# Masks of a stick-breaking attention on TensorE, its steps reordered, and later loads of spilled blocks, in a kernel for one hybrid decoder layer

## The chip, the cores and the metric

One core of one Trainium2 chip runs the whole layer as one program. The metric is the device time of one execution in microseconds (us). The engines are named as in the profile: PE (TensorE, products), PEld (its weight loads), DVE (VectorE), ACT (ScalarE), POOL (GpSimd) and SP (SyncE, which here only issues transfers).

## The reference

The layer works on 512 tokens of 2048 features in float32:

```
h    = RMSNorm(x);  u, v_sgu, q, k, v, g_a, g_b = split(h @ W_in)
y_a  = gelu(u) * (tril(W_s) @ RMSNorm(gelu(v_sgu)) + b)       # chunks of 128 tokens, 8 groups
z    = q k^T * scale                                          # 8 heads of 128, q and k normalised
log_1m = where(strict, log_sigmoid(-z), 0)                    # strict: key before query
tail = reverse cumsum over keys of log_1m, less log_1m itself
w    = where(strict, exp(log_sigmoid(z) + tail), 0);  y_b = w @ v
x   += (sigmoid(g_a) * (y_a @ W_up_a) + sigmoid(g_b) * (y_b @ W_up_b)) @ W_o
x   += (silu(gate) * up) @ W_ffn_out,  gate, up = split(RMSNorm(x) @ W_ffn_in)   # 5632 hidden
x   += sigmoid(RMSNorm(x) @ W_gate) * (p @ W_ple)
```

The mask `strict` acts twice: on log_1m before the cumulative sum, and on w after the exponential.

## The kernel before

Features lie on the 128 partitions and tokens on the free axis, so a *block* is 256 features by 512 tokens, stored as 128 x 1024. A large product reads *units* of 256 input features. Each float32 operand is split into a high part (ACT copies it, rounded, to the type fp32r) and a low part (DVE subtracts the high part), and a product is three products hi x hi, hi x lo, lo x hi in PSUM. Weights: `whi` (ACT, L336) and `wlo` (DVE, L333). Inputs: `parts` (ACT L262, DVE L263). A unit of kind P is plain: twelve PE products of 128 x 512. A unit of kind S uses a Strassen-like scheme with seven small products in place of eight, and wants sums of quarter blocks first (DVE L501; ACT L488 multiplies by the norm's gain). The prepared form of a unit is a *form*.

The stages, in order of time: the form of x and the first q, k and v blocks; the other w_in pairs in four rounds (q, k, v and some gate blocks each), then SGU blocks; the up products and W_o; FFN-in with 44 hidden pairs; FFN-out in three passes over the hidden units (`PASSES`), each of 8 output blocks; the gate stage, with the per-layer embedding. Between stages, blocks are spilled to DRAM: y, gates, x1 (after W_o), hid (hidden units), sum (running FFN-out sums), x2 (after the FFN). The first pair of a stage is done *plain*, unit by unit, while the forms of its inputs are still being made.

All engines' orders are written out by a planner in the kernel. Its clock counts *ticks*, one after each unit of a pair: 8 in a pair of W_in. `after(n, f)` runs f n ticks later; `beside(steps, first)` starts a chain of steps, and each `yield n` in it puts the next step n ticks on. Attention is such a chain, so its instructions stand between the large products. `builds` is the list of forms to be made, whose loads and splits are handed out by the ticks. SBUF for blocks is an arena (`wholes`, float32) with `take` and `give`; `parts` is another arena. A block that is reused is only free for writing when what reads it, a store too, has ended.

Attention for one round has two heads. For each of four query/key chunks j, `stage_a` computes z (L1028), log-sigmoids from Abs, Exp and Ln, and zeroes the masked part of log_1m with a POOL affine_select (L1041). `stage_b` splits it (ACT L262, DVE L263, tile `sp`), multiplies both parts by a triangle of ones `tri` on PE (L1056, L1057: the cumulative sum), takes Exp, and zeroes w with a second select (L1063). `finish` multiplies w by v (L1072). Before it, q_prep, k_prep, v_prep and, for SGU, sgu_v normalise blocks: `times` (L987) scales a transposed block, and a transpose (L965) or a product (L1126) reads it. A pair's output block is put together by ACT and DVE, L691 and L694 (in PSUM's place), in a *home* block; the home of a q block also receives y, which is stored from there.

## Time and profile before

| what | value |
|---|---|
| median of 3 timed runs | 2743.61 us (2743.32 to 2745.96) |
| profiled execution | 2738.06 us, span 2736.3 us |
| PE busy | 2680.7 us (98%), granted clock 0.992 |
| DVE busy | 2168.8 us (79%) |
| ACT busy | 1362.4 us (50%) |
| POOL busy | 443.4 us (16%) |
| moved by DMA | 527.82 MB, mean 193 GB/s |

Stage borders on the profile's clock, to find a window: first products until about 87 us, W_in with attention and SGU to 855, up products and W_o to 1195, FFN-in to 2050, FFN-out passes from about 2050, 2245 and 2395, gate stage from 2550. A row of the windows view gives a stretch's length, then each engine's busy time with its count of instructions in brackets, then the granted clock of PE, the share of busy DMA engines and GB/s. A row of the waits view reads "engine tile line <- engine tile line": the second ended the idle time of the first, with the total, the number of times and the longest.

### The profile page before, as it was taken

The numbers are of one execution on the slowest core, as the hardware profiler recorded it, in microseconds if no ns is written. First come the engines' busy times: TensorE is split into PE (matmuls) and PEld (weight loads), VectorE is DVE, ScalarE is ACT, GpSimd is POOL, SyncE is SP. The second block draws the span as 40 slices with busy tenths as digits, with TensorE's granted clock in tenths as the row PEclk, the third lists the DMA queues.
The fourth block names the chain that finished last, engine by engine and source line by source line (L and its number), as shares of the span: only waits on it lengthen the run. The fifth ranks groups of instructions, "written<-read, shape, count | busy, mean of one in ns | idle before, by whom it ended". The sixth has DMA issues, their size and how long they took to land.

```text
span 2736.3 us, 43138 instructions
## 1 busy us (share of the span) xinstructions
PE 2680.7 (98%) x15875; PEld 2360.9 (86%) x15875; DVE 2168.8 (79%) x3713; ACT 1362.4 (50%) x2142; POOL 443.4 (16%) x503
## 2 busy tenths in 40 slices
PE   8999999999999999999999999999999999999899
PEld 6889888888988889988888888888888989988798
DVE  7687878788887667679898989898988577778676
ACT  7756556565544334365444444444445344444443
POOL 0222222222210000001111111111111111010110
PEclk9999999999999999999999999999999999999999
DMA  6677676767776457668888888888887668777784
GB/s 217 160 187 173 170 178 168 176 163 190 172 178 210 137 156 218 176 197 210 220 214 205 203 203 201 203 202 203 202 202 211 172 186 226 199 238 217 212 235 124
DMA packets 302547, 527.82 MB, mean 193 GB/s; under 512 B 25600, under 2 KB 162816, under 8 KB 302336
## 3 DMA queue, kind: packets, MB, share of 16 engines
q1 hardware_dynamic: 241584, 424.65, 49.6%
q0 software_dynamic: 60752, 100.43, 23.2%
q8 instruction: 124, 2.03, 0.3%
q14 instruction: 87, 0.71, 0.1%
HBM read 477.79 MB, written 47.19 MB: 192 GB/s over the span
## 4 chain that ended last, share of the span: by engine, by line
PE 85%; DVE 5%; DMA 4%; ACT 2%; issue 2%; POOL 1%; ACTq 0%; DVEq 0%; SPq 0%; POOLq 0%
PE ps L648 38%; PE ps L268 13%; PE ps L267 13%; PE ps L269 13%; PE small L648 4%; DVE wlo L333 2%; ACT whi L336 1%; DMA wholes<-w_in 1%; DVE out L694 1%; DVE parts L263 1%; PE small L1072 1%; PE small L965 1%; DMA wholes<-x 1%; DVE wholes L501 1%; DMA wholes<-y 0%
## 5 line engine op out<-in xcount | busy, mean ns | idle before, releaser
L336 ACT ACTIVATE whi<-wholes 128x512 fp32r<-128x512 f32 (+4 forms) x950 | 846.5, 916 | 836.0 <-PE ps L268 317.2
L648 PE MATMUL ps<-parts,whi 128*128 128x512 f32 x3384 | 1132.3, 400 | 5.8 <-DVE wholes L694 4.4
L333 DVE TENSOR_TENSOR wlo<-wholes,whi 128x512 fp32r<-128x512 f32 (+4 forms) x950 | 961.0, 1045 | 97.9 <-ACT whi L336 97.2
L267 PE MATMUL ps<-parts,whi 128*128 128x256 f32 (+1 forms) x2675 | 857.1, 323 | 28.0 <-ACT parts L262 13.9
L268 PE MATMUL ps<-parts,whi 128*128 128x256 f32 (+1 forms) x2640 | 858.1, 325 | 3.1 <-DVE parts L263 3.0
L269 PE MATMUL ps<-parts,wlo 128*128 128x256 f32 (+1 forms) x2640 | 854.4, 324 | 0.9 <-DVE wlo L333 0.9
L648 PEld LDWEIGHTS ps<-parts,wlo 128*128 128x128 f32 x3384 | 637.2, 189 | 145.1 <-DVE wlo L333 1.4
L648 PE MATMUL ps<-parts,wlo 128*128 128x256 f32 x3384 | 673.1, 280 | 0.5 <-DVE wlo L333 0.5
L267 PEld LDWEIGHTS ps<-parts,whi 128*128 128x128 f32 x2675 | 510.0, 191 | 73.6 <-ACT parts L262 17.7
L648 PEld LDWEIGHTS ps<-parts,whi 128*128 128x128 f32 x3384 | 544.1, 190 | 11.0 <-DVE wholes L694 4.8
L268 PEld LDWEIGHTS ps<-parts,whi 128*128 128x128 f32 x2640 | 503.5, 191 | 49.7 <-DVE parts L263 5.7
L269 PEld LDWEIGHTS ps<-parts,wlo 128*128 128x128 f32 x2640 | 503.0, 191 | 39.4 <-DVE wlo L333 1.3
L352 DVE TENSOR_TENSOR wholes<-wholes 128x256 f32<-128x256 f32 (+1 forms) x794 | 328.0, 413 | 22.9 <-issue 3.0
L340 POOL DMA_DIRECT2D wholes<-w_ffn_in x172 | 150.1, 872 | 745.5 <-DMA wholes<-w_ffn_in 183.0
L694 DVE TENSOR_TENSOR out<-out,ps 128x256 f32<-128x256 f32 x373 | 152.8, 420 | 116.4 <-ACT out L691 106.3
L340 POOL DMA_DIRECT2D wholes<-w_in x132 | 117.7, 892 | 541.2 <-DMA wholes<-w_in 226.2
L263 DVE TENSOR_TENSOR parts<-wholes,parts 128x1024 fp32r<-128x1024 f32 (+3 forms) x129 | 122.6, 964 | 28.4 <-ACT parts L262 28.0
L648 PE MATMUL small<-parts,whi 128*128 128x512 f32 x344 | 136.0, 395 | 0.0
L262 ACT ACTIVATE parts<-wholes 128x1024 fp32r<-128x1024 f32 (+3 forms) x129 | 105.6, 845 | 53.1 <-DMA wholes<-hid 24.8
L1335 ACT ACTIVATE out<-out 128x512 f32<-128x512 f32 x44 | 27.9, 635 | 193.8 <-DVE out L1334 193.8
L340 POOL DMA_DIRECT2D wholes<-w_ffn_out x56 | 56.9, 1016 | 406.9 <-DMA wholes<-w_ffn_out 161.6
L662 DVE TENSOR_TENSOR out<-out 128x256 f32<-128x256 f32 x36 | 15.3, 424 | 117.5 <-ACT out L659 117.5
(122 smaller groups left out, 1697.8 us busy)
## 6 DMA issues: line engine op xcount, KB each, us to landing
wholes<-w_ffn_in SPq DMA_DIRECT2D x172, 384.0 KB, 5.6
wholes<-w_in SPq DMA_DIRECT2D x132, 384.0 KB, 4.9
wholes<-w_ffn_in SPq DMA_DIRECT2D x172, 256.0 KB, 4.8
wholes<-w_ffn_in POOLq DMA_DIRECT2D x172, 256.0 KB, 5.4
wholes<-w_in SPq DMA_DIRECT2D x132, 256.0 KB, 3.9
wholes<-w_in POOLq DMA_DIRECT2D x132, 256.0 KB, 5.0
wholes<-w_ffn_out SPq DMA_DIRECT2D x31, 512.0 KB, 4.0
wholes<-x SPq DMA_DIRECT2D x30, 512.0 KB, 4.8
```

The lines of the kernel that those rows point to most:

```text
L262: return (nc.scalar.activation(hi, src, AF.Copy), nc.vector.tensor_tensor(out=lo, in0=src, in1=hi.bitcast(F32), op=ALU.subtract))
L263: nc.vector.tensor_tensor(out=lo, in0=src, in1=hi.bitcast(F32), op=ALU.subtract))
L267: nc.tensor.matmul(ps[:, s], sh, mh[:, s], start=start, stop=False)
L268: nc.tensor.matmul(ps, sh, ml, start=False, stop=False)
L269: return nc.tensor.matmul(ps, sl, mh, start=False, stop=stop)
L333: in_turn(nc.vector.tensor_tensor(out=self.lo[:, blocks], in0=r, in1=h.bitcast(F32), op=ALU.subtract))
L336: in_turn(nc.scalar.activation(h, r, AF.Copy))
L340: nc.gpsimd.dma_start(out=raw[:, 3:5], in_=self.src[:, 1:3], accum_op=ALU.add)
L352: in_turn(nc.vector.tensor_tensor(out=o, in0=x, in1=y, op=ALU.add))
L648: i = nc.tensor.matmul(out, w, t, start=first and k == 0, stop=last and k == 1)
L694: in_turn(nc.vector.tensor_tensor(out=out, in0=x, in1=y, op=op))
L1335: nc.scalar.activation(g, g, AF.Silu)
```

## The change

1. **Masks on PE.** A constant tile `mask` is added (2^99 on the diagonal, -2^99 in row 0). stage_a adds `tri` x `mask` onto the first 128 columns of z in PSUM, which makes masked scores so large and negative that both selects are left out. That is 32 more PE products and 64 fewer POOL selects.
2. **Order of attention.** The split of a sum (`split_sums`) is emitted one step ahead of its products; stage_a(1, 3) starts with the end of head 0, and finish(0) comes a tick later, in the steps of head 1. y is stored per head, in two stores of half a block. q_prep and sgu_v wait 3 ticks instead of 2 before the reader of a scaled block, k_prep 3 before its first head. v_prep and attention start at other ticks. Some scratch tiles lie elsewhere, and y_a blocks are taken from the low end.
3. **Placement.** `take(n, "place")` aligns to n instead of PLACE.
4. **keep_for** keeps a finished block for its form only when that form is the first late one in `builds`.
5. **Loads in mid-pair.** The load of a running sum comes 3 ticks into the pair, that of x1 and of e and x2 in the gate stage 4 ticks in; before, all stood ahead of the pair. The chain of norm3 starts a tick later.

The core of the diff:

```
-                    start = -(-start // PLACE) * PLACE
+                    start = -(-start // n) * n
...
+    hide = wide()[:, :P]
+    nc.vector.tensor_scalar(out=hide, in0=ident, scalar1=HIDE, scalar2=None, op0=ALU.mult)
+    nc.vector.memset(hide[0:1], -HIDE)
+    mask = consts.tile([P, P], F32R, name="mask")
+    nc.scalar.activation(mask, hide, AF.Copy)
...
             times(gv, ps, rr)
-            yield 2
+            yield 3
...
-            nc.tensor.matmul(z, kT[:, c : c + P], qT[:, c : (h + 1) * T], start=True, stop=True)
+            nc.tensor.matmul(z, kT[:, c : c + P], qT[:, c : (h + 1) * T], start=True, stop=False)
+            nc.tensor.matmul(z[:, :P], tri, mask, start=False, stop=True)
...
-            nc.gpsimd.affine_select(out=zs[:, :P], in_=zs[:, :P], pattern=[[1, P]],
-                                    compare_op=ALU.is_gt, fill=0.0, base=0,
-                                    channel_multiplier=-1)
...
+        def split_sums(h, j):
+            n = (NT - j) * P
+            split_into(*(t[:, :n] for t in sp_parts), state[h, j][0])
...
-            nc.gpsimd.affine_select(out=w[:, :P], in_=w[:, :P], pattern=[[1, P]],
-                                    compare_op=ALU.is_gt, fill=0.0, base=0,
-                                    channel_multiplier=-1)
...
+            done = slice(h * T, (h + 1) * T)
+            nc.scalar.activation(qT[:, done], y, AF.Copy)
+            nc.sync.dma_start(out=y_spill[rnd][:, done], in_=qT[:, done])
             if h == 1:
-                nc.sync.dma_start(out=y_spill[rnd], in_=qT)
                 give(y_b[rnd])
...
+        stage_a(0, 3)
         for h in range(2):
             yield 2
+            for j in range(NT - 1, 0, -1):
+                split_sums(h, j)
+                stage_a(h, j - 1)
+                yield 1
+                stage_b(h, j)
+                yield 1
             yield 1
+            split_sums(h, 0)
             yield 1
+            stage_b(h, 0)
             yield 1
+            if h == 0:
+                stage_a(1, 3)
+                after(1, lambda: finish(0))
+            else:
+                yield 1
+                finish(1)
...
-            beside(v_prep(o, v))
-            beside(attention(i, qT, kT, rk, v), 5)
+            beside(v_prep(o, v), 1 if i else 6)
+            beside(attention(i, qT, kT, rk, v), 3 if i else 13)
...
-        if j < KU - KEPT or form.raw or not fits([(wholes, 1024, "low")] * 2):
+        late = [f for f in builds if f.fetches and f.ready()]
+        if (j < KU - KEPT or form.raw or late and late[0] is not form
+                or not fits([(wholes, 1024, "low")] * 2)):
             give(block)
...
-            before = load(spill["sum", j]) if c else None
-            x1 = load(spill["x1", j]) if c == len(PASSES) - 1 else None
+            if c:
+                after(3, lambda f=fetch: f("sum"))
+            if c == len(PASSES) - 1:
+                after(4, lambda f=fetch: f("x1"))
             pr = pair(units, last=j == KU - 1, plain=j == 0, at=first)
...
-        e, x2 = load(ple_spill[j]), load(spill["x2", j])
+        after(4, fetch)
```

Three places in the written-out order, before and then with the change. A row is the number in its engine's order, the line, the operation, and output <- inputs with the shape.

First PE, in round 1 of attention, at the end of head 0: from the last product with `tri` (L1057, L1068 with the change) to the product with v (L1072, L1080). Before:

```order
1374 L1057 MATMUL small_246_2837<-sp1_132,tri_122 128x512
1375 L648 MATMUL ps_252_2890<-parts_73,whi0_76 128x512
1376 L648 MATMUL ps_249_2870<-parts_73,whi2_80 128x512
1377 L648 MATMUL ps_249_2870<-parts_73,wlo2_81 128x256 x2
1378 L648 MATMUL ps_249_2870<-parts_73,whi2_80 128x512
1379 L648 MATMUL ps_250_2875<-parts_73,whi2_80 128x512
1380 L648 MATMUL ps_250_2875<-parts_73,wlo2_81 128x256
1381 L648 MATMUL ps_255_2901<-parts_73,whi0_76 128x512
1382 L648 MATMUL ps_255_2901<-parts_73,wlo0_77 128x256 x2
1383 L1072 MATMUL small_253_2895<-wholes_74 128x512
```

With the change (the first half of the way):

```order
1351 L1068 MATMUL small_251_2795<-sp1_137,tri_122 128x512
1352 L649 MATMUL ps_238_2649<-parts_73,whi1_78 128x512
1353 L649 MATMUL ps_239_2654<-parts_73,whi1_78 128x512
1354 L649 MATMUL ps_239_2654<-parts_73,wlo1_79 128x256 x2
1355 L649 MATMUL ps_239_2654<-parts_73,whi1_78 128x512
1356 L649 MATMUL ps_240_2664<-parts_73,whi1_78 128x512
1357 L649 MATMUL ps_240_2664<-parts_73,wlo1_79 128x256 x2
1358 L649 MATMUL ps_240_2664<-parts_73,whi1_78 128x512
1359 L1038 MATMUL small_255_2837<-wholes_74 128x128
1360 L1039 MATMUL small_255_2837<-mask_127,tri_122 128x128
```

Before, nine rows lie between the two; with the change the first score product of head 1 (1359) and its mask product (1360) come in between, and L1080 follows at row 1376.

Second SP, at the end of W_o and the first pair of the FFN; x1_727 to x1_734 before, x1_744 to x1_751 with the change, are blocks 0 to 7 of x1. Before:

```order
428 L1316 DMA x1_733_9255<-wholes_74 128x1024
429 L316 DMA wholes_74<-w_ple 128x512 x3
430 L484 DMA wholes_74<-x1_730_9252 128x1024
431 L316 DMA wholes_74<-w_ffn_in 128x1024
432 L484 DMA wholes_74<-x1_731_9253 128x1024
433 L316 DMA wholes_74<-w_ffn_in 128x1024
434 L1316 DMA x1_734_9256<-wholes_74 128x1024
435 L821 DMA ple_875_10723<-out_872_10706 128x1024
436 L316 DMA wholes_74<-w_ffn_in 128x1024
437 L821 DMA ple_882_10745<-out_879_10728 128x1024
438 L316 DMA wholes_74<-w_ffn_in 128x1024
439 L484 DMA wholes_74<-x1_733_9255 128x1024
```

With the change:

```order
451 L822 DMA ple_906_10790<-out_903_10773 128x1024
452 L319 DMA wholes_74<-w_ffn_in 128x2x256
453 L321 DMA wholes_74<-w_ffn_in 128x768
454 L485 DMA wholes_74<-x1_749_9231 128x1024
455 L485 DMA wholes_74<-x1_750_9232 128x1024
456 L319 DMA wholes_74<-w_ffn_in 128x2x256
457 L321 DMA wholes_74<-w_ffn_in 128x768
458 L485 DMA wholes_74<-x1_751_9233 128x1024
```

Before, block 5 is a kept one, block 6 is loaded behind the last store of x1 (439) and block 7 ten rows later (449); with the change blocks 5, 6 and 7 are loaded close together, 14 to 18 rows behind the last store of x1 (440).

Third SP, at the border to the gate stage; x2_743 to x2_750 before, x2_760 to x2_767 with the change, are blocks 0 to 7 of x2. Before:

```order
1059 L1373 DMA x2_750_9272<-wholes_74 128x1024
1060 L484 DMA wholes_74<-x2_743_9265 128x1024
1061 L316 DMA wholes_74<-w_gate 128x4x128
1062 L484 DMA wholes_74<-x2_746_9268 128x1024
1063 L318 DMA wholes_74<-w_gate 128x2x256
1064 L484 DMA wholes_74<-x2_749_9271 128x1024
1065 L484 DMA wholes_74<-x2_747_9269 128x1024
1066 L316 DMA wholes_74<-w_gate 128x1024
1067 L484 DMA wholes_74<-x2_750_9272 128x1024
```

With the change:

```order
1063 L485 DMA wholes_74<-x2_765_9247 128x1024
1064 L319 DMA wholes_74<-w_gate 128x2x128
1065 L321 DMA wholes_74<-w_gate 128x3x128
1066 L319 DMA wholes_74<-w_gate 128x2x256
1067 L1394 DMA x2_767_9249<-wholes_74 128x1024
1068 L317 DMA wholes_74<-w_gate 128x4x128
1069 L319 DMA wholes_74<-w_gate 128x2x256
1070 L485 DMA wholes_74<-x2_766_9248 128x1024
1071 L485 DMA wholes_74<-x2_767_9249 128x1024
1072 L485 DMA wholes_74<-ple_3_107 128x1024
1073 L485 DMA wholes_74<-x2_760_9242 128x1024
```

Before, the load of x2_0 for the end of the first pair (1060) and then blocks 3, 6, 4 and 7 follow the last store; with the change only blocks 6 and 7 do, and that of x2_0 stands behind them (1073).

More of the change, by code (lines that the diff above doesn't have):

```diff
@@ L948, in a_tiles @@
     def a_tiles(*tags):
-        for tag, n in (("l", T), ("own", 5 * P), ("w0", T), ("w1", 3 * P), ("w2", 2 * P), ("w3", P),
-                       ("k", 1024), ("v", 1024), ("zs", 1024)):
+        for tag, n, how in (("l", T, "high"), ("w0", T, "high"), ("w1", 3 * P, "high"),
+                            ("w2", 2 * P, "high"), ("k", 1024, "low"), ("v", 1024, "low"),
+                            ("zs", T + 3 * P, "tight"), ("own", 5 * P, "tight"),
+                            ("w3", 2 * P, "tight")):
             if (tag in "kv") == ("k" in tags):
-                att[tag] = take(n)
+                att[tag] = take(n, how)
     def a_tile(tag, n=T, start=0):
@@ L968, in squares @@
     def squares(ps):
[L970 removed]
+        ms, junk = small(NT), tmp.tile([P, P], F32, tag="sq", name=nm("sq"), bufs=1)
         for t in range(NT):
@@ L999, in q_prep @@
             yield 1
-            times(q.f(), ps, r)
-            yield 2
-            nc.scalar.activation(s, flip(q.f()), AF.Copy, scale=gcol[:, g_q : g_q + 1])
-            give(q)
+            times(qn, ps, r)
+            yield 3
+            nc.scalar.activation(s, flip(qn), AF.Copy, scale=gcol[:, g_q : g_q + 1])
+            if q:
+                give(q)
     def k_prep(o, rk):
         for h in range(2):
-            yield 2
+            yield 3 - h
             token_rms(flip(o[:, h * T : (h + 1) * T]), rk[:, NT * h : NT * (h + 1)])
@@ L1158, in block @@
         if w == "s":
-            y_a[i] = take(1024, "high")
+            y_a[i] = take(1024)
             return y_a[i].f()
@@ L1359, in hybrid_layer, with fetch @@
         for j in range(KU):
-            before = load(spill["sum", j]) if c else None
-            x1 = load(spill["x1", j]) if c == len(PASSES) - 1 else None
+            got = {}
+            def fetch(*names, got=got, j=j):
+                for n in names:
+                    got[n] = load(spill[n, j])
+            if c:
+                after(3, lambda f=fetch: f("sum"))
+            if c == len(PASSES) - 1:
+                after(4, lambda f=fetch: f("x1"))
             pr = pair(units, last=j == KU - 1, plain=j == 0, at=first)
+            before, x1 = got.get("sum"), got.get("x1")
             if before is None:
@@ L1379, in hybrid_layer, with fetch @@
             give(before)
-    after(2, norm3.chain.step)
+    after(3, norm3.chain.step)
     give(norm2.block)
     for j in range(KU):
-        e, x2 = load(ple_spill[j]), load(spill["x2", j])
+        blocks = []
+        def fetch(blocks=blocks, j=j):
+            blocks.extend((load(ple_spill[j]), load(spill["x2", j])))
+        after(4, fetch)
         def finish(o, a, b, ps=None):
@@ L1400, in finish @@
             nc.scalar.activation(s, s, AF.Sigmoid)
+            e, x2 = blocks
             nc.vector.tensor_tensor(out=s, in0=s, in1=e.f(a, b), op=ALU.mult)
@@ L1410, in hybrid_layer @@
             finish(o, 0, 2 * T)
-            give(e, x2)
+            give(*blocks)
     finish_waiting()
```

27 lines of the change are left out of this document (6 added, 21 removed).

## The prediction

> **What bounds the kernel now.** I read the page's first part, the table of PE's waits, and then time windows at the borders of the stages.
>
> ```profile
> span 2736.3 us, 43138 instructions
> PE 2680.7 (98%) x15875; PEld 2360.9 (86%) x15875; DVE 2168.8 (79%) x3713; ACT 1362.4 (50%) x2142; POOL 443.4 (16%) x503
> ```
>
> PE is the bound with 98%. The profiled execution took 2738.06 us, 1.8 more than its span and 5.55 below the median of the timed runs (2743.61). The change removes no product of the layer, so it can win only what PE loses: 2736.3 - 2680.7 = 55.6 us of idleness, and time at a lower clock. The windows say where (us, busy time and count of PE, PEld, DVE, ACT, POOL, then PE's granted clock, DMA share, GB/s).
>
> ```profile
> 87.00:855.00 768.00, 751.10 (x4692) 662.18 (x4690) 617.88 (x1166) 453.54 (x922) 194.17 (x225) 0.99 0.71 177
> 1195.00:1240.00 45.00, 43.99 (x213) 35.62 (x212) 38.80 (x68) 37.45 (x55) 6.95 (x8) 1.00 0.81 240
> 1240.00:2050.00 810.00, 810.00 (x4653) 706.79 (x4652) 733.45 (x1330) 383.12 (x542) 144.68 (x166) 1.00 0.84 206
> 2050.00:2130.00 80.00, 76.63 (x460) 67.85 (x459) 65.09 (x114) 40.25 (x56) 9.84 (x10) 1.00 0.72 201
> 2245.00:2295.00 50.00, 46.97 (x298) 42.23 (x297) 39.45 (x68) 21.74 (x33) 7.75 (x8) 0.97 0.87 244
> 2395.00:2420.00 25.00, 21.07 (x98) 17.84 (x96) 15.40 (x23) 8.29 (x12) 3.02 (x3) 0.86 0.82 241
> 2550.00:2580.00 30.00, 17.92 (x86) 14.23 (x85) 19.10 (x37) 13.24 (x19) 4.20 (x4) 0.77 0.65 184
> ```
>
> PE idles 768 - 751.1 = 16.9 us beside attention and SGU, 1.0 at the start of the FFN, nothing in its body (some 43 pairs of 8 ticks in 810 us, so a tick is about 2.4 us), 3.4, 3.0 and 3.9 at the starts of the three FFN-out passes, and 12.1 at the start of the gate stage. What ended these waits (in total, times, longest):
>
> ```profile
> PE ps L267 <- ACT parts L262: 13.9, 3, 9.5
> PE small L1126 <- ACT wholes L987: 4.4, 3, 2.1
> PE ps L648 <- DVE wholes L694: 4.4, 2, 2.6
> PE small L1072 <- POOL wholes L1063: 3.3, 3, 1.7
> PE ps L268 <- DVE parts L263: 3.0, 3, 2.1
> ```
>
> A wait costs more than itself, where the granted clock falls after it:
>
> ```profile
> 340.00:360.00 20.00, 17.43 (x99) 14.96 (x99) 12.86 (x23) 7.19 (x11) 1.75 (x2) 0.91 0.64 164
> 480.00:500.00 20.00, 18.21 (x105) 15.69 (x104) 13.60 (x26) 7.53 (x13) 1.93 (x3) 0.91 0.65 167
> 660.00:680.00 20.00, 18.14 (x110) 16.45 (x109) 13.09 (x25) 9.98 (x27) 6.44 (x7) 0.91 0.65 149
> 770.00:790.00 20.00, 17.87 (x110) 16.14 (x109) 12.81 (x26) 9.47 (x26) 5.09 (x7) 0.91 0.65 163
> 2060.00:2080.00 20.00, 17.59 (x89) 14.68 (x88) 19.86 (x40) 12.96 (x18) 1.73 (x2) 1.00 0.63 165
> 2254.49 0.43 PE ps L267
> 1228.83 0.23 PE ps L268
> ```
>
> The last two rows are pieces of the chain of waits: the same product of 128x512 takes 0.43 us just after a wait and 0.23 elsewhere. Four 20 us windows of the attention stage stand at 0.91, that is 0.09 x 20 = 1.8 us each. They follow the two waits on L694 and two of those on L987, all of about 2 us. Not every such wait does it (2060:2080 holds 2.4 us of idleness at 1.00).
>
> The Trainium skill ("TensorE: Matmul & The Clock Gate", the part on the HAM clock gate) has the clock fall after at least one idle window of about 3.4 us, and says the window runs freely. By that alone the waits of 2 us would cost no clock. The trace shows 0.91 behind them, so I follow the trace; the other sum is a rival below.
>
> **Attention and SGU (87 to 855).** Its prices:
>
> ```profile
> L1063 POOL TENSOR_SCALAR_AFFINE_SELECT wholes<-wholes 128x128 f32<-128x128 f32 x32 | 33.9, 1059 | 12.5 <-ACT wholes L1062 12.5
> L1041 POOL TENSOR_SCALAR_AFFINE_SELECT wholes<-wholes 128x128 f32<-128x128 f32 x32 | 12.9, 404 | 45.3 <-DVE wholes L1039 45.2
> L1056 PE MATMUL small<-sp,tri 128*128 128x128 f32 x8 | 2.0, 249 | 0.0
> L1057 PE MATMUL small<-sp,tri 128*128 128x128 f32 x8 | 2.4, 300 | 0.0
> 342.84 3.84 DMA y<-wholes
> ```
>
> Removed: 64 POOL selects, 33.9 + 12.9 us of POOL. POOL is not the bound; what counts is that 1.06 us of L1063 stood between the last Exp and L1072 (3.3 us of waits), and that finish(0) now comes after a step of head 1. Each SGU or q step before a transposed product gets one tick more, about 2.4 us against a longest wait of 2.1: the waits on L987 go, 4.4 us and two clock falls (3.6). The copy L691/L694 into a q home waited for the store of y out of the same block (3.84 us); y is now stored per head, half the bytes, the first half a head earlier, and the home is taken later: 4.4 us and two falls (3.6). Together 3.3 + 8.0 + 8.0 = 19.3. Splits ahead of stage_b save most of the small waits of the tri products, some 1.7 more: 21.
>
> Added: 32 mask products on PE. Lower bound a quarter of the 0.23 us of a 512-column product, 32 x 0.058 = 1.8 us; upper bound the busy time of L1057 of this size, 32 x 0.300 = 9.6, which includes the tail that overlaps the next product. I take 3.5, nearer the lower. New waits: in round 0 one q home now stands close behind its store (up to 2.6 us with half the bytes in flight), and a few splits remain close to their reader. I take 3.5 for these (0 to 8). Gain: 21 - 7 = **14** (6 to 20).
>
> **Start of the FFN (1195 to 1240): a loss.** keep_for now keeps a block only when its form is next in line, and in the program as it is written out that is never so: loads from x go from 30 to 32.
>
> ```profile
> wholes<-x SPq DMA_DIRECT2D x30, 512.0 KB, 4.8
> 1211.18 9.06 DMA wholes<-x
> L488 ACT ACTIVATE wholes<-wholes,gcol 128x512 f32<-128x512 f32 x42 | 28.7, 716 | 14.5 <-DMA wholes<-x 9.7 <-DMA wholes<-xT 4.8
> L501 DVE TENSOR_TENSOR wholes<-wholes 128x256 f32<-128x256 f32 x136 | 53.0, 419 | 9.4 <-ACT wholes L488 8.8 <-PE small L898 0.4
> L263 DVE TENSOR_TENSOR parts<-wholes,parts 128x1024 fp32r<-128x1024 f32 x57 | 69.2, 1220 | 20.7 <-ACT parts L262 20.3
> L263 DVE TENSOR_TENSOR parts<-wholes,parts 128x768 fp32r<-128x768 f32 x34 | 32.4, 953 | 4.1 <-ACT parts L262 4.0
> ```
>
> Before, three units of x1 were split ahead of the first pair and five inside it; in the new order it is one and seven. A unit costs DVE 1.22 + 0.95 + 4 x 0.42 = 3.85 us, so 7.7 us move into a stretch where DVE is busy 38.8 of 45 us: 6.2 us are free, and not all at the right place. From 1.5 to 7.7 us of this is late. Beside it x1_5, x1_6 and x1_7 are loaded inside the first pair where only x1_7 was (9.06 us to landing). ACT works in the order of its list, so the gain of one unit (2 x 0.72) that waits for its load holds back the split of the one before. Both are one delay, not a sum. With a clock fall of 1.8 I take **6** lost (1.5 to 10).
>
> **Starts of the passes.**
>
> ```profile
> 2241.61 7.45 DMA wholes<-hid
> 2399.77 6.42 DMA sum<-wholes
> 2406.20 4.06 DMA wholes<-hid
> ```
>
> Pass 1: the last hid block was issued 8.8 us ahead of PE's need (from the order and PE's durations) and took 7.45, and after it come ACT and DVE. Now it is issued about 15 us ahead, because the load of the sum stands in mid-pair. The whole loss goes: 3.0 idle and 0.03 x 50 = 1.5 of clock, **4.5**. Pass 2: the hid load went into the block whose sum was just being stored, so it waited 6.42 us for that store, and was issued 4.3 us ahead of its use. Now the last is 7.9 us ahead and follows no store: 3.9 idle and a clock fall (0.14 x 25 = 3.5, part of it while idle; I take 2.7), of which 0.8 stays: **5.8**. Pass 0: DVE is busy 19.86 of 20 us at 2060 and its splits stay; I take **1.5** lost (0 to 3) because its order gets slightly tighter.
>
> **Start of the gate stage.**
>
> ```profile
> 2555.89 7.05 DMA wholes<-x
> 2572.14 1.50 DVE wlo L333
> ```
>
> The load of 2555.89 is behind the last x2 store and the finish load of x2_0; PE waited 9.5 us for it. Four x2 blocks were loaded there; now x2_3, x2_4 and x2_5 come in the last pass, and only x2_6 and x2_7 stay, 7 and 9 us ahead of their use, with the finish loads behind them. The loss now is 12.1 idle plus clock: 0.23 x 30 = 6.9 us of clock, twice that at half rate, 9.5 of it idle, so 4.3 us busy at half rate, 2.2 lost. Of 14.3 I leave 3.5 for a load of 7.05 plus its split, and for a wlo like the one of 2572.14 that ends late. Gain **10.8** (6 to 13).
>
> **Sum:** 14 + 4.5 + 5.8 + 10.8 - 6 - 1.5 = 27.6 us. On the profile's time 2710.5, on the median 2743.6 - 27.6 = **2716**.
>
> **Rivals.**
> - *The FFN start costs nothing* (DVE's 6.2 free us and the weights prepared ahead absorb it): 27.6 + 7.5 = 35, 2708.5. For it: PE idled only 1.0 there. Against: DVE's 86% and a 9.06 us load. 0.14.
> - *Attention's waits come back in other steps*, since its chain keeps ACT and DVE steps of 0.7 us each and mask products at their upper price: attention brings 4, not 14, 2726. 0.12.
> - *The clock falls only after some 3.4 us.* Then 7.2 us of clock in attention and 1.5 in pass 1 are not this change's to win, 2725. Against: 0.91 behind four short waits. 0.04. The Trainium skill's page named above reads so.
> - *The moved loads stand where they hold up as much as before*, and the gains at gate and passes (21) are given back at the FFN start: within 0.2% of before, 2741. 0.07.
> - *Slower: late loads land one after another.* At the FFN start three x1 loads in turn at 9.06 end 27 us after the first issue, which is 10 us ahead of use, and need 5 us of ACT and DVE behind: 22 lost instead of 6, and two x2 loads at the gate likewise lose its 10.8, two clock falls more (3.6): 2716 + 16 + 10.8 + 3.6 = 2746.5; with the mask products at 9.6 instead of 3.5, 2752. It decides from 9 us for each load in series. Against: 4.8 us is the median of 30 such loads, and 244 GB/s is moved at once. 0.07.
>
> **Numbers.** The forecast has 0.56, with its own range 2707 to 2726; the rest as above. Range for 8 in 10: 2701 to 2734, from the better end of attention and the FFN start to the attention rival with the FFN start at its worst. A measurement can tell about 0.2%, 5.5 us: faster 0.56 + 0.14 + 0.12 + 0.04 = 0.86, same 0.07, slower 0.07.
>
> **What would show it.** Rows of PE waiting for the q home (L694), for the normalised blocks (L987) and for a POOL select (L1063) are gone, under whatever line they then have, and 20 us windows of attention at 1.00; PE's idleness over attention near 7 us. At the start of the FFN more idleness than 1.0, ended by splits of x1 or an x load. At pass 1 and 2 no wait over 1 us, at the gate 3 to 4 us in place of 12.1. It is wrong if attention still idles over 12 us, or the FFN start loses over 10.

## The result, and the profile after

The changed kernel takes 2721.11 us (median of 5 runs, 2720.11 to 2728.73) where the kernel before takes 2743.61: 22.5 us less, a ratio of 0.9925 with a 95% interval of 0.9907 to 0.9943. The forecast was 2716, with a range of 2701 to 2734. The profiled execution took 2728.73 us, the longest of the five, and that of before (2738.06) is shorter than all five timed runs now known of it (2738.29 to 2746.59). The two profiles alone would show 9.3 us, so wherever a few microseconds matter below, several profiles of the same code stand side by side.

The page's first rows of the changed kernel:

```profile
span 2726.8 us, 43175 instructions
PE 2678.1 (98%) x15907; PEld 2360.1 (87%) x15907; DVE 2163.1 (79%) x3715; ACT 1354.3 (50%) x2143; POOL 394.5 (14%) x439
```

The same windows as in the prediction (length, busy time and count of PE, PEld, DVE, ACT, POOL, granted clock, DMA share, GB/s), without that of the FFN body:

```profile
87.00:855.00 768.00, 751.24 (x4735) 663.51 (x4735) 615.31 (x1169) 445.37 (x922) 144.69 (x161) 1.00 0.71 178
1195.00:1240.00 45.00, 40.86 (x169) 32.19 (x167) 34.92 (x59) 36.15 (x52) 6.38 (x6) 0.92 0.79 242
2050.00:2130.00 80.00, 76.66 (x441) 66.94 (x440) 72.89 (x128) 44.19 (x62) 9.47 (x10) 1.00 0.75 206
2245.00:2295.00 50.00, 49.06 (x285) 43.07 (x284) 41.58 (x69) 24.18 (x35) 8.65 (x9) 1.00 0.92 260
2395.00:2420.00 25.00, 24.32 (x114) 20.05 (x113) 21.45 (x31) 12.31 (x16) 3.31 (x3) 1.00 0.91 292
2550.00:2580.00 30.00, 27.18 (x146) 22.61 (x145) 27.37 (x48) 19.16 (x31) 5.56 (x5) 1.00 0.94 287
```

At the gate stage PE's idleness falls from 12.1 to 2.8 us and the clock rises from 0.77 to 1.00; pass 1 goes from 3.0 to 0.9, pass 2 from 3.9 to 0.7. Attention idles as much as before, 16.8 us (16.9), though its clock is 1.00 now. The start of the FFN has become worse: 4.1 us and a clock of 0.92 (1.0 and 1.00). PE's waits of the whole run (in total, times, longest) say what is new:

```profile
PE ps L268 <- ACT parts L263: 5.8, 3, 3.8
PE ps L649 <- DVE p L695: 4.6, 6, 1.7
PE small L973 <- ACT wholes L995: 3.1, 5, 1.4
PE small L973 <- ACT sq L980: 2.6, 4, 1.5
PE ps L269 <- DVE parts L264: 2.4, 5, 0.7
```

No wait on a POOL select is left, and the q home (L695 into `wholes`) has 1.8 us. In their place PE waits for DVE to empty a PSUM bank (tile p, L695), for the token norms of q and k (squares of L980, scaled blocks of L995, read by the transposes of L973), and for forms (L263, L264). The longest of the first row, 3.8 us, ends at 858 us, the start of the up products; from the chain of waits around it and at the start of the FFN:

```profile
850.07 7.08 DMA wholes<-y
1215.79 8.23 DMA wholes<-x
```

The last load of y took 7.08 us, and at the start of the FFN a load of x1 took 8.23, issued after two weight loads that stood ahead of it in SP's order.

To see stages apart from the shifts of whole traces, I cut each trace at the same instructions: the ends of the 19th, 355th, 403rd and 943rd of the 965 DVE combines of L694 (L695 or the like in the others). "Attention" runs from the first to the second, "up to FFN body" (up products, W_o, the FFN's first pair) to the third, the FFN body to the fourth, "rest" (passes and gate stage) to the end of the span. All in us, one profiled execution each:

```
kernel         attention   up to FFN body   FFN body   rest    span
before           701.5         446.4          758.2    687.0   2736.3
changed          700.8         457.4          758.2    665.8   2726.8
after_again      699.0         452.6          758.8    665.6   2719.0
attn_only        697.5         450.1          758.3    678.7   2726.6
loads_only       704.5         445.2          758.8    662.9   2716.7
old_keep         699.7         451.5          758.3    665.5   2717.9
no_mask          697.5         455.2          759.5    665.2   2720.5
pool_mask        714.9         453.2          759.3    667.9   2738.1
pool_keep_n1     713.8         445.8          758.2    667.2   2727.7
loads_ticks      706.0         446.9          758.3    666.3   2721.5
keep_n1          701.3         445.7          758.3    666.1   2713.8
loads_pemask     701.4         445.2          758.2    663.8   2711.0
pemask_y         695.6         445.4          758.8    664.5   2706.3
old_attn         705.0         447.8          758.2    667.9   2725.0
```

The FFN body, which no edit touches, is the same to 1.3 us in all of them, so the cuts are good to about that. The other columns are less steady: attention, with the same code, spreads by up to 4 (701.5, 704.5 and 705.0 for the old one; 700.8, 699.0, 697.5, 699.7 and 701.3 for the new one with masks on PE).

### The profile page after: what moved, and what is told of

Read it like the earlier page. It is cut to its first block, busy times and chain, and to the rows that moved or that the text cites. A ratio compares the mean times of both kernels' runs of the same rounds, so it can differ in the third digit from the quotient of the medians.

```text
span 2726.8 us, 43175 instructions
## 1 busy us (share of the span) xinstructions
PE 2678.1 (98%) x15907; PEld 2360.1 (87%) x15907; DVE 2163.1 (79%) x3715; ACT 1354.3 (50%) x2143; POOL 394.5 (14%) x439
## 4 chain that ended last, share of the span: by engine, by line
PE 83%; DVE 7%; DMA 4%; ACT 3%; issue 2%; POOL 1%; SPq 0%; DVEq 0%; ACTq 0%; POOLq 0%
PE ps L649 36%; PE ps L269 14%; PE ps L270 14%; PE ps L268 14%; PE small L649 4%; DVE wlo L334 3%; DMA wholes<-w_in 1%; ACT whi L337 1%; DVE out L695 1%; DVE wholes L695 1%; PE small L1080 1%; DVE wholes L353 1%; PE small L1038 1%; DMA wholes<-y 1%; DMA wholes<-x 1%
## 5 line engine op out<-in xcount | busy, mean ns | idle before, releaser
L695 DVE TENSOR_TENSOR out<-out,ps 128x256 f32<-128x256 f32 x373 | 152.4, 419 | 122.8 <-ACT out L692 112.9
L264 DVE TENSOR_TENSOR parts<-wholes,parts 128x1024 fp32r<-128x1024 f32 (+3 forms) x129 | 122.5, 961 | 31.8 <-ACT parts L263 31.6
L263 ACT ACTIVATE parts<-wholes 128x1024 fp32r<-128x1024 f32 (+3 forms) x129 | 105.4, 844 | 49.5 <-DMA wholes<-hid 19.3
```

The source lines that it names most:

```text
L263: return (nc.scalar.activation(hi, src, AF.Copy), nc.vector.tensor_tensor(out=lo, in0=src, in1=hi.bitcast(F32), op=ALU.subtract))
L264: nc.vector.tensor_tensor(out=lo, in0=src, in1=hi.bitcast(F32), op=ALU.subtract))
L695: in_turn(nc.vector.tensor_tensor(out=out, in0=x, in1=y, op=op))
```

## The experiments

Theory after the first profile: the moved loads bring all of the gain, attention brings little since its waits have moved, and the start of the FFN costs 6 to 11 us. The rival: attention brings its 14 us, and the profile fell on an unlucky execution. All ratios are to runs of the kernel before on the same chip; they are not quotients of the medians given here, and differ from these by up to 0.002.

### The changed kernel again, and its parts

after_again is the changed kernel without an edit.

> The changed kernel once more, for a second profile beside the first (2728.7 us, the longest of its five executions; the others 2720.1 to 2724.4). If the waits of the first profile are the kernel's own, the same rows come back: about 15 us of PE idleness in attention, a wait near 3.8 us at the start of the up products (about 858 us), 4 us of idleness and a granted clock near 0.92 at the start of the FFN, and the total is 2718 to 2729. If they were chance of that execution, one or more of them is gone (the load of y lands in under 5 us instead of 7.08, the clock in the FFN's first 45 us is above 0.96), and the execution is some 4 to 8 us shorter.

Measured: 2722.13 us, ratio 0.9931 (0.9912 to 0.9950); before 2738.78. Part came back and part did not. Attention idles 16.4 us (768 - 751.58) and the FFN start 4.4 us (45 - 40.63), so these belong to the kernel:

```profile
87.00:855.00 768.00, 751.58 (x4738) 663.18 (x4737) 617.42 (x1170) 445.54 (x922) 144.66 (x161) 1.00 0.71 179
1195.00:1240.00 45.00, 40.63 (x182) 31.75 (x181) 40.09 (x71) 37.06 (x53) 6.42 (x7) 0.96 0.72 217
```

The wait for y at the up products is 0.6 us here, not 3.8 (the last load of y lands in 4.80 us, not 7.08), so its size is chance. That there is one is less so: in the other profiles of the new order it is 0.6 to 2.6 us, in those of the old order 0.3 to 1.1.

attn_only has the attention hunks and the placement alone. Beside the changed kernel:

```
-        late = [f for f in builds if f.fetches and f.ready()]
-        if (j < KU - KEPT or form.raw or late and late[0] is not form
-                or not fits([(wholes, 1024, "low")] * 2)):
+        if j < KU - KEPT or form.raw or not fits([(wholes, 1024, "low")] * 2):
...
-                after(3, lambda f=fetch: f("sum"))
...
+            before = load(spill["sum", j]) if c else None
...
-        after(4, fetch)
+        e, x2 = load(ple_spill[j]), load(spill["x2", j])
```

> The kernel before with the attention part of the change alone (masks on PE, splits a step ahead, heads overlapped, y stored per head, placement); keep_for and the loads as before. By the prediction it wins 14 us: median near 2729.5. By what the first profile of the change shows (idleness of attention 16.8 us as before, but no fall of the clock save one, mask products to pay) it wins 0 to 7: 2737 to 2744, with PE waiting in attention on the transposes (token norms) and on blocks put together by DVE in place of the old waits. In either case the start of the passes and of the gate stage lose what they lost before.

Measured: 2732.84, ratio 0.9976 (0.9961 to 0.9992), 5.9 under before, and not 14. By the table it wins 4.0 in attention and loses 3.7 up to the FFN body. One thing was not expected: 8.3 us are won in the rest without any moved load. The wait of pass 2 is gone, as these windows show; the gate stage still waits. In this run SP issues the last hid load of pass 2 at 2392.26, ahead of the store of a sum at 2399.43; before, it came at 2406.20, behind that store. Whether the placement or another attention hunk brings this about was not separated.

```profile
2395.00:2420.00 25.00, 25.00 (x143) 21.99 (x142) 20.82 (x32) 10.10 (x15) 3.03 (x3) 1.00 0.97 319
2550.00:2580.00 30.00, 21.88 (x108) 17.96 (x109) 18.10 (x34) 15.23 (x23) 1.31 (x3) 0.83 0.63 193
```

loads_only is the kernel before with the hunks of `fetch` and the later start of norm3 alone.

```
-            before = load(spill["sum", j]) if c else None
...
+            if c:
+                after(3, lambda f=fetch: f("sum"))
...
-        e, x2 = load(ple_spill[j]), load(spill["x2", j])
+        after(4, fetch)
```

> The kernel before with the loads of sums, x1, x2 and of the per-layer embedding in mid-pair alone; attention and keep_for as before. By the prediction's terms for pass 1, pass 2 and gate it wins 21 us: near 2722.5, with under 1.5 us of idleness at each of the three places, and the FFN start stays as it was (1.0 us idle). A rival: the loads only come earlier because no block is kept any more (one x2 block less in the arena's way); then this kernel wins under 10 us (over 2734) and the wait at the gate stage stays over 5 us.

Measured: 2720.79, ratio 0.9928 (0.9907 to 0.9950), 18.0 under before: nearly all of the change's gain by itself. The rest takes 662.9 in place of 687.0 us, and the wait of 9.5 us at the gate stage is gone:

```profile
2245.00:2295.00 50.00, 48.16 (x308) 43.57 (x308) 40.03 (x68) 22.79 (x34) 7.74 (x8) 1.00 0.91 261
2550.00:2580.00 30.00, 29.34 (x187) 26.31 (x186) 24.57 (x46) 17.82 (x25) 9.32 (x6) 1.00 1.01 310
```

So the rival that the loads only come early because no block is kept falls: keep_for is the old one here.

### What the start of the FFN costs

old_keep is the changed kernel with the old keep_for (the first four lines of the diff of attn_only).

> The changed kernel with the old keep_for, so that block 5 of x1 is kept again and two x1 blocks are loaded behind the last store, not three. If the loss at the start of the FFN (first profile: 4.1 us idle, clock 0.92 over 45 us; 11 us later on the body of the FFN than before) is the price of keep_for, the FFN body starts 6 to 8 us earlier and the median is 6 to 8 us under the changed kernel's (about 2714). If that loss comes from the traffic and from the order of the splits, it stays: within 2 us of the changed kernel.

Measured: 2719.11, ratio 0.9920 (0.9901 to 0.9940), 3.0 under after_again, between the two expectations. The stretch up to the FFN body is still 451.5 us. The wait has only changed its name: PE now stands 3.4 us for the norm's diagonals (L878), which DVE makes behind the sums of a late block. From the chain of waits:

```profile
1212.89 8.42 DMA wholes<-x
1222.85 0.67 DVE wholes L502 x2
1223.52 0.21 DVE out L878
1223.77 0.49 PE small L920 x2
```

old_attn prices keep_for from the other side: the changed kernel with the attention hunks undone.

```
-        stage_a(0, 3)
         for h in range(2):
+            stage_a(h, 3)
             yield 2
...
-            nc.tensor.matmul(z[:, :P], tri, mask, start=False, stop=True)
...
+            nc.gpsimd.affine_select(out=w[:, :P], in_=w[:, :P], pattern=[[1, P]],
+                                    compare_op=ALU.is_gt, fill=0.0, base=0,
+                                    channel_multiplier=-1)
```

> The changed kernel with the attention part undone: new keep_for, placement and loads over the old attention with masks on POOL. Beside the loads alone (2720.8; FFN start and up stage 445.1 us from the end of attention to the FFN's body, as in the kernel before) this prices keep_for by itself. If keep_for is what costs the FFN start, that stretch is 450 to 455 us and the median 5 to 8 us over the loads alone (2726 to 2729). If the loss at the FFN start came from where attention left the arena and the norm's diagonals behind a late load, the stretch is 445 to 448 and the median within 2 us of the loads alone.

Measured: 2723.96, ratio 0.9946 (0.9925 to 0.9967). The stretch is 447.8 us, 2.6 over loads_only; the new placement is in this run too, so the 2.6 are its and keep_for's together. From after_again to old_keep, which differ by keep_for alone, it is 1.1 in the same stretch and 3.0 in the medians. So keep_for costs some 1 to 3 us; the attention part with the placement cost 3.7 (450.1 - 446.4). Together they cost 6.2 and 11.0 (452.6 and 457.4; the second holds the wait of 3.8 us for y).

The expectation looked at that stretch alone, but the rest is longer too, 667.9 in place of 662.9 us: PE waits 2.2 us at once for splits at the start of pass 1 and a fall of the clock follows (0.93 in the window 2245:2295, in loads_only 1.00), though the loads are moved as there. So the moved loads do not remove the wait of pass 1 whatever the rest does; why it is back here was not tried.

### The masks

In the profiles of the change a mask product seems to take long:

```profile
L1039 PE MATMUL small<-mask,tri 128*128 128x128 f32 x32 | 14.8, 464 | 0.0
```

From its start to the next product's start 0.30 us pass in the median, 9.6 in all. no_mask leaves both masks out, so that the record can be compared with one without the product.

```
-            nc.tensor.matmul(z, kT[:, c : c + P], qT[:, c : (h + 1) * T], start=True, stop=False)
-            nc.tensor.matmul(z[:, :P], tri, mask, start=False, stop=True)
+            nc.tensor.matmul(z, kT[:, c : c + P], qT[:, c : (h + 1) * T], start=True, stop=True)
```

> The changed kernel without any mask in attention: neither the 32 mask products nor POOL selects, so attention is not causal here; all else as changed. In the profiles of the change each mask product holds PE 0.30 us from its start to the next product's (median; 9.63 us in all 32), where the prediction took 0.11 (3.5 in all). If PE's time is what they cost, this kernel is 9 to 10 us under the changed one (2712 to 2713 where that has 2722). If the price was as predicted, or their time lies inside waits that stay, it is 2 to 4 us under (2718 to 2720).

Measured: 2720.43, ratio 0.9928 (0.9910 to 0.9946), 1.7 under after_again. My reading of the record was wrong and the prediction's price right. The timelines of PE at the same place say why. Without the mask product (first fence), then with it (second):

```profile
133.80 0.39 PE L1033 MATMUL small<-wholes 128*128 128x128 f32 x2
133.94 0.48 PE L649 MATMUL ps<-parts,whi 128*128 128x512 f32 x1
134.25 0.40 PE L649 MATMUL ps<-parts,wlo 128*128 128x256 f32 x2
```

```profile
133.73 0.39 PE L1038 MATMUL small<-wholes 128*128 128x128 f32 x2
133.87 0.30 PE L1039 MATMUL small<-mask,tri 128*128 128x128 f32 x1
134.01 0.45 PE L649 MATMUL ps<-parts,whi 128*128 128x512 f32 x1
134.30 0.39 PE L649 MATMUL ps<-parts,wlo 128*128 128x256 f32 x2
```

The float32 score product is recorded twice, and whatever comes next starts in the record right behind the start of the second of the two: the large product of 128x512, elsewhere 0.23 us from its start to the next start, has 0.31 here (133.94 to 134.25), and 0.63 behind the widest score product. With the mask in between, the mask's record bears that time. So the price must be read over the whole group, from the start of the score product to the end of the large product's turn: 0.45 us without the mask (133.80 to 134.25), 0.57 with it (133.73 to 134.30). The difference is 0.11 to 0.12 us for each of the four widths of the scores (medians), some 3.6 us for all 32.

Attention less its idleness is 687.1 us in after_again and 684.5 in no_mask, 2.6 us apart, but that measure cannot carry a price: in pool_mask (below), which has no mask product either, it is 691.7, with one fall of the clock.

pool_mask puts the selects back on POOL in the new order.

```
-            nc.tensor.matmul(z[:, :P], tri, mask, start=False, stop=True)
+            nc.gpsimd.affine_select(out=zs[:, :P], in_=zs[:, :P], pattern=[[1, P]],
+                                    compare_op=ALU.is_gt, fill=0.0, base=0,
+                                    channel_multiplier=-1)
...
             nc.scalar.activation(w, w, AF.Exp)
+            nc.gpsimd.affine_select(out=w[:, :P], in_=w[:, :P], pattern=[[1, P]],
+                                    compare_op=ALU.is_gt, fill=0.0, base=0,
+                                    channel_multiplier=-1)
```

> The changed kernel with the masks back on POOL (two selects for each step, no mask product); order of steps, y stores, keep_for and loads as changed. If the new order hides the selects (the product with v stands 17 to 25 rows of PE's order behind the last tri product, before 9 to 20), the masks on PE were a pure loss and this kernel is 6 to 9 us under the changed one (2713 to 2716). If the selects hold up the product with v again, waits of PE on POOL of 3 to 6 us in all come back with falls of the clock, and it stands within 2 us of the changed kernel or above it.

Measured: 2738.98, ratio 0.9992 (0.9978 to 1.0006): 17 us over the changed kernel. The second case allows that by its "or above it", but PE's waits on POOL are far from 17 us, and the clock falls only once in attention, at its beginning. Attention takes 714.9 us. PE's and DVE's waits between 87 and 855 us:

```profile
PE ps L649 <- DVE p L695: 10.3, 12, 2.3
PE small L1080 <- POOL wholes L1071: 4.9, 5, 1.1
DVE wholes L1051 <- POOL wholes L1046: 15.4, 17, 2.7
```

And DVE's in the kernel before, in the old order:

```profile
DVE wholes L1046 <- POOL wholes L1041: 6.9, 18, 1.6
```

The product with v waits 4.9 us for POOL. More costly is DVE: it waits 15.4 us in L1051 for the first select (6.9 before), and PE waits 10.3 us on L695, whose combine stands in the same DVE order; that the one makes the other is read from the order, not tried. So the new order of attention needs the masks on PE: by itself it loses (714.9, and 713.8 in pool_keep_n1 below, against 701.5 to 705.0).

loads_pemask is the counterpart: the old order of attention with the masks on PE (on top of loads_only; the scratch of the squares in one buffer, for room).

```
-            nc.tensor.matmul(z, kT[:, c : c + P], qT[:, c : (h + 1) * T], start=True, stop=True)
+            nc.tensor.matmul(z, kT[:, c : c + P], qT[:, c : (h + 1) * T], start=True, stop=False)
+            nc.tensor.matmul(z[:, :P], tri, mask, start=False, stop=True)
...
-            nc.gpsimd.affine_select(out=zs[:, :P], in_=zs[:, :P], pattern=[[1, P]],
...
-            nc.gpsimd.affine_select(out=w[:, :P], in_=w[:, :P], pattern=[[1, P]],
...
```

> The kernel before with the loads in mid-pair and the masks on PE alone, in the old order of attention (the squares' scratch goes to one buffer, for room). In the profiles a mask product seems to hold PE 0.30 us, but its record takes in the second pass of the score product before it; from the run without masks the price is (687.2 - 684.7) / 32 = 0.08 us each, 2.5 in all. In the profile of the loads alone PE waited 6.1 us for POOL selects. If the masks on PE are worth their price in the old order, these waits go and the median is 3 to 6 us under that of the loads alone (2715 to 2718 where that has 2721). If each cost 0.30 us, or the old order's waits on POOL only change to waits on ACT's Exp, it stands at 2720 or above.

Measured: 2711.98, ratio 0.9906 (0.9889 to 0.9924), 8.8 under loads_only's 2720.79, more than the 3 to 6 expected, though that was timed on another occasion: by the ratios the step is 0.9928 to 0.9906, some 6 us. It also beats the changed kernel (its six runs take 2709.94 to 2719.70, those of after_again 2719.93 to 2724.81). The POOL waits of 6.1 us (loads_only, first row) are gone, and what remains in loads_pemask are the q home and the scaled blocks:

```profile
PE small L1072 <- POOL wholes L1063: 6.1, 2, 3.0
```

```profile
PE small L1127 <- ACT wholes L993: 5.2, 3, 2.5
PE ps L649 <- DVE wholes L695: 5.0, 2, 4.0
```

### The small edits

loads_ticks adds only the third tick in q_prep and sgu_v to loads_only.

```
             times(q.f(), ps, r)
-            yield 2
+            yield 3
...
             times(gv, ps, rr)
-            yield 2
+            yield 3
```

> The kernel before with the loads in mid-pair, and the third tick before the reader of a scaled block in q_prep and sgu_v, the one small part of the attention change that only waits longer. In the profile of the loads alone PE waited 4.6 + 2.1 us on these blocks, and the clock fell behind some of it. If that part does what the prediction says by itself, the waits on ACT L987 go and the median is 6 to 9 us under that of the loads alone (2712 to 2715 where that has 2721). If the delay only moves other steps into waits, it stays within 3 us of it.

Measured: 2725.37, ratio 0.9953 (0.9935 to 0.9972), no gain: 4.6 over loads_only, a little more than the 3 us allowed, with runs that overlap. PE's waits of SGU on L987 are 4.6 us, as they were. Those of the transposes on L987 went from 2.1 to 0.4, and 4.5 us for the squares of the token norms are new:

```profile
PE small L1126 <- ACT wholes L987: 4.6, 4, 2.5
PE small L965 <- ACT sq L972: 4.5, 3, 1.9
```

pool_keep_n1 was to be a version that beats both: POOL masks, the old keep_for, and the FFN norm's chain a tick earlier.

```
-    after(2, norm2.chain.step)
+    after(1, norm2.chain.step)
```

> A version meant to beat both: the changed kernel with masks on POOL, the old keep_for, and the chain of the FFN norm started 1 tick on rather than 2, so that its diagonals stand ahead of the sums of the late x1 unit on DVE (with the old keep_for alone PE waited 3.4 us there for diagonals behind a load that took 8.4 us). Expected by theory: 3 us for keep_for, 6 to 9 for the masks, 3 for the norm: 2707 to 2711 where the changed kernel has 2722. If the late x1 load itself is what PE waits for, whoever stands behind it, the wait only changes its name at the FFN start and the sum is 2710 to 2714; if the masks on POOL cost as much as on PE, 2716 or more.

Measured: 2729.67, ratio 0.9961 (0.9946 to 0.9975). It loses by its POOL masks (attention 713.8). But up to the FFN body it takes 445.8, so keep_n1 puts the same two edits on the changed kernel with masks on PE.

> The changed kernel (masks on PE) with the old keep_for and the chain of the FFN norm one tick on instead of two: the last version meant to beat both. With POOL masks the same two edits brought the stretch from the end of attention to the body of the FFN down from 452.7 us (changed kernel, second profile) to 445.8 and its idleness at the FFN start from 4.4 to 1.0 us. If these edits add to the rest, idleness between 1195 and 1240 is near 1 us and the median is 7 us under the changed kernel (about 2715 where that has 2722), 3 to 5 under the version with the old keep_for alone (2719). If the wait at the FFN start depends on how far attention shifted the rest, it stays within 2 us of that version.

Measured: 2717.91, ratio 0.9923 (0.9905 to 0.9941). The FFN start idles 0.15 us, as expected; the median is 4.2 under after_again, not 7, and by the ratios, since before was timed anew, only some 2. The windows of old_keep and of keep_n1:

```profile
1195.00:1240.00 45.00, 41.63 (x195) 34.43 (x194) 35.57 (x60) 31.01 (x46) 7.34 (x8) 0.96 0.82 240
```

```profile
1195.00:1240.00 45.00, 44.85 (x223) 37.46 (x222) 38.74 (x65) 33.21 (x49) 7.18 (x8) 1.00 0.88 260
```

pemask_y takes loads_pemask and stores y per head, in half stores.

```
+            done = slice(h * T, (h + 1) * T)
+            nc.scalar.activation(qT[:, done], y, AF.Copy)
+            nc.sync.dma_start(out=y_spill[rnd][:, done], in_=qT[:, done])
             if h == 1:
-                nc.sync.dma_start(out=y_spill[rnd], in_=qT)
```

> The kernel before with the loads in mid-pair, masks on PE (old order of attention), and y stored per head in two half stores. In the profile without the last edit PE waited 4.1 and 0.9 us for the home of a q block behind the store of y (5.8 and 2.6 us to landing), and the clock fell to 0.83 in that window. If the wait is the landing of 512 KB, a half store lands earlier by 1 to 3 us: median 2 to 5 us under that version (2707 to 2710 where that has 2712). If a store's landing is set by latency and by the traffic beside it rather than by its size, the wait stays within 1 us and so does the median.

Measured: 2707.50, ratio 0.9888 (0.9865 to 0.9912), the fastest version: 4.5 under loads_pemask, as expected, and none of its four runs is as long as the shortest there. The wait for the q home shrinks from 5.0 to 1.6 us (first row below), and the window that had 0.83 in loads_pemask (second fence) has 1.00:

```profile
PE ps L649 <- DVE wholes L695: 1.6, 2, 1.5
480.00:500.00 20.00, 18.23 (x119) 16.06 (x119) 14.17 (x24) 8.17 (x17) 1.72 (x2) 1.00 0.56 141
```

```profile
480.00:500.00 20.00, 15.95 (x81) 13.49 (x80) 10.36 (x21) 4.99 (x9) 1.74 (x2) 0.83 0.54 134
```

That half the bytes land sooner explains only a part. At the longer of these waits the half store took 4.54 us and the whole one 5.77, 1.2 less, where the wait is 2.6 shorter; and over all stores of y the medians are 3.0 us for 256 KB and 2.9 for 512 KB. And loads_pemask has two more falls of the clock (0.91 at 360:380 and 660:680), behind waits of other kinds of 2.8 and 2.5 us; pemask_y has such waits too (2.6, 2.2 and 2.1 us) and no fall behind them. How much of the 4.5 us the half stores bring is therefore open.

## Why the prediction was right, and where it was not

The direction and the range were right; 2721.11 is 5.1 over the forecast. The forecast's own signs of being wrong came true all the same: attention still idles over 12 us (16.8 and 16.4), and the FFN start loses over 10 in one of two profiles (11.0 and 6.2). So the time was met by the moved loads and a wide range, and not by the account of attention. By its steps:

- **Passes 1, 2, 0 and gate: right in sum.** Predicted -4.5 (pass 1), -5.8 (pass 2), +1.5 (pass 0) and -10.8 (gate), together -19.6; the stretch of passes and gate went from 687.0 to 665.8 and 665.6, that is -21.3, and loads_only shows -24.1. Pass 0 did not get worse (3.3 us idle as before). Two things the forecast did not see. The wait of pass 2 goes where the last hid load no longer stands behind the store of a sum, and attn_only has that without any moved load, so there the gains of the two parts overlap and cannot be added. And moved loads do not settle the wait: old_attn has that of pass 1 again, and in after_again PE still waits 1.3 us at once at pass 2, behind a hid load of 7.89 us.
- **Masks, 3.5 us: right** (3.6 by the timelines; leaving them out won 1.7 in the medians).
- **Waits that attention loses, 21 us: right in the main.** The waits on POOL, on the q home and of SGU on L987 went from 3.3, 4.4 and 4.4 us to 0, 1.0 to 1.8 and 0.7, those of the tri products on their splits from 1.7 to 0.2, and the four clock falls of attention to one and none.
- **The step that failed is "new waits, 3.5 us (0 to 8)".** These are after_again's waits of PE between 87 and 855 us:

```profile
PE ps L649 <- DVE p L695: 6.2, 8, 1.7
PE small L973 <- ACT sq L980: 2.5, 4, 1.5
PE small L973 <- ACT wholes L995: 2.2, 4, 1.1
PE ps L649 <- DVE out L695: 1.3, 3, 0.5
PE ps L649 <- DVE wholes L695: 1.0, 3, 0.5
PE small L1136 <- ACT wholes L995: 0.7, 2, 0.5
```

  The first four rows are 12.2 us together, where the kernel before has 1.9 for the like (0.5, 0, 0.5 and 0.9): 10.3 us of new waits in place of 3.5. With these, and with 1.9 us that stayed of the old waits, the forecast's terms give 21 - 1.9 - 3.5 - 10.3, some 5 us. So attention idles nearly as before, and the stage wins 4.0 us (mean of the five profiles of the new code with masks on PE, 699.7, to that of the three of the old, 703.7), not 14. The first of these waits is a q home again, in round 0, whose copy waited for a half store that took 6.00 us to land, and behind which two halves of a weight split (2.00 us) stood ahead of the combine that PE needed:

```profile
207.03 6.00 DMA y<-wholes
214.31 2.00 DVE wlo L334 x2
216.31 0.33 DVE p L695
```

  The forecast had seen this home as up to 2.6 us, with half the bytes in flight, and not what DVE does in order behind it. Nor did half the bytes land sooner: in the two profiles of the changed kernel the half stores of y took 3.1 to 7.0 us, the whole ones before 2.8 to 3.8. The Trainium skill ("TensorE: Matmul & The Clock Gate", Part 1, on engine queue depths) says that ACT and DVE are strict first-in-first-out queues; the trace agrees, in 2.00 us of splits ahead of a 0.33 us combine.
- **A tick more, so that "the waits on L987 go", 8 us: wrong by itself.** loads_ticks shows that edit alone leaving SGU's waits and adding some for the squares. In the change SGU's waits on that line went, but the transposes of q and k wait 3.1 and 2.2 us on it (L995 there), 0.5 before; what took SGU's away was the order as a whole, and which line of it, I did not separate.
- **FFN start, 6 us lost: size right in after_again (6.2), above the range in the first profile (11.0), cause half right.** As foretold, splits of x1 end the waits, behind a load of x (8.23 us above). But keep_for is only some 1 to 3 us of it; the other part is attention's with the placement: without the new keep_for (old_keep, attn_only), a late x1 block stands before the norm's diagonals on DVE. With the old keep_for and the norm's chain a tick earlier together the stretch falls to 445.7 (keep_n1); the norm's tick with the new keep_for was not tried.
- **Clock falls after waits of 2 us:** see below; the forecast priced all of the old ones at 1.8 us, and in attention the change's profiles have one and none.

Put together, the stretches give -4.0 - 21.3 + 6.2 = -19.1 us where the forecast had -27.6: 10 us of attention are missing, and the loads brought 1.7 more. The medians gave -22.5 on the first occasion and -16.7 on the second. That the total came so near is in part luck: the median of the kernel before was higher on the first occasion (2743.61) than on the four later ones (2737.19 to 2742.13).

The rival that attention's waits come back in other steps (2726, given 0.12) describes the waits better than the likeliest case did, though its mask products at their upper price are not what the timelines show; its time is as far above the first median as the forecast is below it. The rivals "the FFN start costs nothing", "the moved loads hold up as much as before" (whose 2741 does not follow from its terms: 2716 + 21 is 2737) and "slower" all fall with the table. The rival on the clock cannot be told by its time, 2725; the falls behind short waits in the kernel before speak against it.

## What to carry to other kernels

A wait that is moved a step later in an in-order program is not removed until the work queued behind it has been priced: look at which instruction stands behind it on DVE and ACT, and who waits for that one. Of a change with several parts, the one that moves loads away from the border of a stage may bring nearly all of it; here the moved loads and the mask products on PE were each worth keeping and the reordering was not needed: the old order of attention and the old keep_for with these two and half stores of y take 2707.5 us, 10 to 14 less than the change (by the ratios and by the medians). A record's length is not a price: leave the operation out and compare the same group of instructions from start to start.

## What the runs showed of the hardware

A wait near 2 us may or may not cost clock. In the kernel before, four of the five longest waits in attention, 1.66 to 2.57 us, had a 20 us window at 0.91 with them (rows in the prediction); in pemask_y all 20 us windows of attention stand at 1.00 though PE waited up to 2.6 us at a time:

```profile
PE small L1128 <- ACT wholes L993: 5.1, 3, 2.2
PE small L971 <- ACT wholes L993: 3.9, 2, 2.6
```

Each fall in attention lasted 3.41 us in the record or twice that, at half the clock, and whether one followed was not a matter of length alone: a wait of 2.62 us in pemask_y had none, one of 1.79 us in the kernel before had one.

The Trainium skill ("TensorE: Matmul & The Clock Gate", the part on what is happening at the clock gate) gives an idle window of about 3.4 us that runs freely. The free running would agree with falls by chance. But waits of 1.79 and 1.86 us, well under that window, had falls behind them in the kernel before; there the measurement decides.

A float32 product takes time that the record gives to the product behind it (0.31 in place of 0.23 us for 128x512 behind the narrowest score product, 0.63 behind the widest). The landing of one and the same load changes from execution to execution: the last load of y took 7.08 us in one profile of the changed kernel and 4.80 in the other, and PE waited 3.8 and 0.6 us for it.
